# One Silu on ScalarE in place of a tanh and a VectorE product, for the gates of both layers

## The chip, the cores and the metric

The kernel runs on one core of a Trainium2 chip. The metric is the time of one execution on the device, in microseconds (us). A second source is one execution under the hardware profiler: its span goes from the first to the last instruction of the program, and all rows with durations come from it. The engines are called as the profile calls them: PE (TensorE's matmuls; PEld its weight loads), DVE (VectorE), ACT (ScalarE), POOL (GpSimd) and SP (SyncE, which issues the DMAs).

## The reference

Two layers, each a residual: x + W_out(mixer(RMSNorm(x)) * silu(gate)), on 256 positions of width 2048. The gate comes from the layer's one input projection, so it carries the row's norm factor as the other projections do.

```python
def mla_layer(x, ...):                       # layer A
    z = rms_norm(x, norm_g) @ w_in
    cq, ckv, k_pe, gate = jnp.split(z, ...)
    ...
    o = mla_attend(q, k, v, pos)             # 16 heads, softmax with a chunk-causal mask
    return x + (o * jax.nn.silu(gate)) @ w_out

def diff_layer(x, ...):                      # layer B
    z = rms_norm(x, norm_g) @ w_in
    q, k, v, gate = jnp.split(z, ...)
    ...
    o = diff_attend(q, k, v, pos, lam)       # 8 heads, difference of two softmaxes
    o = rms_norm(o, subln_g) * (1.0 - lam_init)
    return x + (o * jax.nn.silu(gate)) @ w_out
```

silu(g) = g * sigmoid(g) = (g / 2) * (1 + tanh(g / 2)).

## The kernel before, in words

The 256 rows are two tiles of 128. All products are made in three matmuls of split operands (mm3, lines 122 to 125): a high part, rounded to the fp32r type, and a low part, the remainder. Weights are streamed from HBM in chunks of two contraction tiles of 128 rows (project, line 127). For each chunk (stream, line 105) a DMA fills `raw`, ACT casts it into `whi` (line 118), and DVE subtracts to give `wlo` (line 119); PE then runs 12 matmuls on the chunk. There are four buffers of `raw` and three each of `whi` and `wlo`, so ACT can cast a chunk only once PE has finished with the one three before it.

The row's norm factor (r0 in layer A, r1x in layer B) is not applied to x. It is applied to what comes out of the projections. The gate's accumulator in PSUM holds g / r0. Before the change, ACT computes tanh(acc * r0h) with r0h = r0 / 2 (line 354 in layer A, line 668 in layer B), DVE adds one and multiplies by the accumulator (lines 355 and 669), and the factor r0h that is still missing enters elsewhere: in layer A in the scaling of the softmax by the reciprocal of its sum (line 474, its second scalar per row), in layer B in the factor f that scales the heads' output (line 722).

Layer A works on pairs of heads (hp = 0 to 7). For each: k_up and q_up project keys, values and queries, head_t transposes them, soft_a makes the scores and the softmax (DVE takes the row's extreme at line 468, ACT the Exp at line 470, DVE the scaling at line 474), p_a transposes the probabilities `e` (line 484), av_a multiplies by the values and by the transposed gate. In between, fill(i) puts chunks of the gate's projection, gate_mm, or of the output projection. The gate has four blocks (gb = 0 to 3) of 512 columns; each ends with the two activations of line 354, one for each row tile, and gate_t transposes the result later. Block 0 is finished ahead of the first softmax, blocks 1, 2 and 3 behind the last chunk put into pairs 0, 2 and 4.

Layer B works on 8 heads. For each: qk_b projects queries and keys, vg_b values and gate (eight chunks), and within vg_b's chunks stand qk_t, soft_b (scores, Exp at line 688, scaling at lines 690 to 692) and p_b, which transposes the probabilities `eb` (line 703). Behind the last chunk of vg_b come the values' split (line 151, tiles vhb and vlb) and the gate's two activations (line 668). av_b and go_b follow among the chunks of the next head's qk_b.

The program gives the instructions in this order, but each engine's own order is settled by the tile framework when it schedules the program: the Exp of line 619, for one, is written behind layer A and runs during its first projection. Each engine runs its list in order. The profile has two table loads on ACT (ACT_TABLE_LOAD): one that line 77 asks for by name, and one at line 619 that the program does not write and the framework put in.

Of the kernel before, what the change touches and what calls it, by code (L numbers as in the profile page):

```python
# [9 lines left out]
F32 = mybir.dt.float32  # L10
# [3 lines left out]
AF = mybir.ActivationFunctionType  # L14
ALU = mybir.AluOpType
# [3 lines left out]
P = 128  # L19
S = 256  # L20
NT = S // P
# [15 lines left out]
BV = 256  # L37
# [17 lines left out]
def hybrid_kernel(ctx: ExitStack, tc: tile.TileContext, x, xT, pos, posc, rows, gains, wz, wgA, wqu, wkvu, woA, wB, woB, out):  # L55
# [18 lines left out]

# [1 line left out]
    gains_t = const.tile([P, 2 * KD + 14], F32, tag="gains", name="gains_t")  # L76
# [16 lines left out]

    # keep the tensor engine's clock up while the first operands arrive
    wsrc = const.tile([P, 512], BF16, tag="wsrc", name="wsrc")
# [4 lines left out]

# [1 line left out]
    state = {}  # L102
# [24 lines left out]
    def project(accs, lhs, blocks, w, c0, c1, nk):  # L127
        """accs[b][t] += lhs(k, t) . weights of block b, for the chunks c0..c1 of two contraction tiles each."""
        for c in range(c0, c1):
            ws = [stream(b[c], 2 * w) for b in blocks]  # L130
            for kk in range(2):
                k = 2 * c + kk
                for (hi, lo), acc in zip(ws, accs):
                    for t in range(NT):
                        xh, xl = lhs(k, t)
                        mm3(acc[t], xh, xl, hi[:, kk * w:(kk + 1) * w], lo[:, kk * w:(kk + 1) * w],
                            k == 0, k == nk - 1)
# [7 lines left out]

# [1 line left out]
    xh = big.tile([P, KD, S], F32R, tag="xh", name="xh")  # L147
# [49 lines left out]

    # mean square of each row of x, and its root's reciprocal
    r0 = const.tile([P, NT], F32, tag="r0", name="r0")
# [9 lines left out]
    rsqrt(r0, msx)  # L209
    r0h = const.tile([P, NT], F32, tag="r0h", name="r0h")  # L210
    V.tensor_scalar(r0h, r0, 0.5, None, ALU.mult)
    r0sq = const.tile([P, NT], F32, tag="r0sq", name="r0sq")
    V.reciprocal(r0sq, msx)

# [1 line left out]
    posr_t = prow[:, 0, :]  # L216
# [25 lines left out]
    A.activation(cos_, kk_, AF.Sin)  # L242
    # ropc[q|k]: cosines, rops: signed sines, both times the gain of the element they multiply
    V.tensor_scalar(gqkr_t[:, 1, :], gqkr_t[:, 1, :], math.sqrt(AQK), None, ALU.mult)
# [31 lines left out]

    # lambda, on every partition
    lamp = sm.tile([P, 2, HD], F32, tag="junk", name="lamp", bufs=1)
# [5 lines left out]

# [1 line left out]
    m16 = big.tile([P, 2, 2, 4, S], F32R, tag="m16", name="m16")  # L286
# [5 lines left out]
    def latents():  # L292
        ss = sm.tile([P, NT, 2, 2], F32, tag="ssl", name="ss", bufs=1)
        for t in range(NT):
            junk = sm.tile([P, 512], F32, tag="junk", name="junk", bufs=1)
            for i in range(2):
                for j, (b, c0, w, o0) in enumerate(pieces[i]):
                    A.activation(junk[:, :w], zacc[b][t][:, c0:c0 + w], AF.Square, accum_out=ss[:, t, i, j:j + 1])
        mean = sm.tile([P, NT, 2], F32, tag="ml", name="mean", bufs=1)
        V.tensor_reduce(mean, ss, AX.X, ALU.add)  # L300
        V.tensor_tensor(mean, mean, bc(r0sq, 2), ALU.mult)
        V.tensor_scalar(mean, mean, 1.0 / LORA, EPS, ALU.mult, ALU.add)
        sig = sm.tile([P, NT, 2], F32, tag="sig", name="sig", bufs=1)
        rsqrt(sig.rearrange("p a b -> p (a b)"), mean.rearrange("p a b -> p (a b)"))
        V.tensor_tensor(sig, sig, bc(r0, 2), ALU.mult)
        for t in range(NT):
            cn = att.tile([P, 2, LORA], F32, tag="gT", name="cn")
            for i in (1, 0):
                for b, c0, w, o0 in pieces[i]:
                    V.tensor_scalar(cn[:, i, o0:o0 + w], zacc[b][t][:, c0:c0 + w], sig[:, t, i:i + 1], None, ALU.mult)  # L310
            cns.append(cn)
        # shared rotary key: its square sum, and its rotated form with the gain
        kp = sm.tile([P, NT, ROPE], F32, tag="kp", name="kp", bufs=1)
        k2 = sm.tile([P, NT, ROPE], F32, tag="k2", name="k2", bufs=1)
        for t in range(NT):
            V.tensor_scalar(kp[:, t], zacc[2][t][:, 256:320], r0[:, t:t + 1], None, ALU.mult)
            junk = sm.tile([P, 512], F32, tag="junk", name="junk", bufs=1)
            A.activation(junk[:, :ROPE], kp[:, t], AF.Square, accum_out=sskp[:, t:t + 1])
        V.tensor_tensor(krope, kp, ropc[:, 1], ALU.mult)
        V.tensor_tensor(k2[:, :, :HR], kp[:, :, HR:], rops[:, 1, :, :HR], ALU.mult)  # L320
        V.tensor_tensor(k2[:, :, HR:], kp[:, :, :HR], rops[:, 1, :, HR:], ALU.mult)
        V.tensor_tensor(krope, krope, k2, ALU.add)
        V.tensor_scalar(sskp, sskp, AQK * EPS, None, ALU.add)
# [15 lines left out]

# [1 line left out]
    KC = KD // 2  # L341
# [4 lines left out]
    def gate_mm(gb, c0, c1):  # L346
        if c0 == 0:
            gate_acc(gb)
        project([state["ga", gb]], feat(xh, xl), [wgA[gb]], 512, c0, c1, KD)
        if c1 == KC:  # L350
            sgs = []
            for t, acc in enumerate(state.pop(("ga", gb))):
                sg = sm.tile([P, 512], F32, tag="sg", name="sg", bufs=2)
                A.activation(sg, acc, AF.Tanh, scale=r0h[:, t:t + 1])
                V.scalar_tensor_tensor(sg, sg, 1.0, acc, ALU.add, ALU.mult)
                sgs.append(sg)
            state["sg", gb] = sgs
# [10 lines left out]
    def k_up(hp):  # L368
        """keys, normalised, and values of two heads"""
        ka = pair(psu)  # L370
# [23 lines left out]
    def q_up(hp):  # L394
        """queries of two heads, not scaled: their norm enters with the scores"""
        kn, rt, ss, f, vh, vl = state["k", hp]
# [25 lines left out]
    def head_t(hp):  # L422
        kn, rt, ss, f, vh, vl = state.pop(("k", hp))
        qn = state.pop(("q", hp))
        tiles = []
# [10 lines left out]
        for i in (1, 0):  # L436
            for t in range(NT):
                T.transpose(pt[:, i, t * P:(t + 1) * P], rt[:, i, t].rearrange("p h d -> p (h d)"), ident)
        # each head's rotary rows: q as [hi; lo], k's hi and lo twice over, so that every product has 128 rows
        q2 = att.tile([P, 2, S], F32R, tag="q2", name="q2")  # L440
# [12 lines left out]
    def soft_a(hp):  # L453
# [9 lines left out]
        for h, ps in enumerate(pss):  # L463
            e = sm.tile([P, NT, S], F32, tag="e", name="e", bufs=2)
            mx = sm.tile([P, NT], F32, tag="mx", name="mx")
            den = sm.tile([P, NT], F32, tag="den", name="den")
            for t in range(NT):
                V.tensor_tensor_reduce(e[:, t, :], ps[:, t, :], maskA[:, t, :], f[:, 0, t, h:h + 1], 3e38,
                                       ALU.add, ALU.min, mx[:, t:t + 1])
                A.activation(e[:, t, :], e[:, t, :], AF.Exp, bias=mx[:, t:t + 1], scale=-1.0,  # L470
                             accum_out=den[:, t:t + 1])
            V.reciprocal(den, den)
            for t in range(NT):
                V.tensor_scalar(e[:, t, :], e[:, t, :], den[:, t:t + 1], r0h[:, t:t + 1], ALU.mult, ALU.mult)
            es.append(e)
# [81 lines left out]

# [1 line left out]
    x1 = big.tile([P, NT, D], F32, tag="m16", name="x1")  # L559
# [56 lines left out]
    rsqrt(r1x, m1)  # L616
    r1h = const.tile([P, NT], F32, tag="r1h", name="r1h")
    V.tensor_scalar(r1h, r1x, 0.5, None, ALU.mult)
    A.activation(lams, lams, AF.Exp)
# [5 lines left out]

# [1 line left out]
    def qk_b(h, c0, c1):  # L627
# [30 lines left out]
    def vg_b(h, c0, c1):  # L658
# [8 lines left out]
        for t in range(NT):  # L667
            A.activation(sg[:, t, :], acc[t][:, BV:], AF.Tanh, scale=r1h[:, t:t + 1])
            V.scalar_tensor_tensor(sg[:, t, :], sg[:, t, :], 1.0, acc[t][:, BV:], ALU.add, ALU.mult)
        state["vgb", h] = (vh, vl, sg)  # L670
# [36 lines left out]
    def av_b(h):  # L707
# [13 lines left out]
        rsqrt(f, ss)  # L721
        V.tensor_tensor(f, f, r1h, ALU.mult)
        go = att.tile([P, NT, BV], F32, tag="go", name="gob", bufs=1)
# [35 lines left out]

# [1 line left out]
    def finish_b(n, t, c0, c1):  # L761
# [20 lines left out]
def _columns(w, width):  # L782
    """(K, N) -> (N / width, K / 256, 128, 2 * width): blocks of columns in chunks of two row tiles."""
    k, n = w.shape
# [48 lines left out]
```

## Time and profile before

| | |
|---|---|
| time, median of 3 runs (lowest, highest) | 847.49 us (846.46, 847.53) |
| span of the profiled execution (its own time beside it is not given) | 845.0 us |
| instructions | 11706 |
| PE busy | 835.9 us, 99% of the span |
| DVE busy | 564.6 us, 67% |
| ACT busy | 488.0 us, 58% |
| POOL busy | 86.4 us, 10% |
| read from and written to HBM | 145.73 MB and 2.10 MB |

A row of the groups by line gives line, engine, operation, tiles written <- read, their shapes and the count, then the busy time in us and the mean of one in ns, and last the engine's idle time just before them and what ended most of it. A row of a timeline gives the start in us from the span's beginning, the duration in us, engine, line, operation, tiles and count (consecutive instructions of a kind are one row), and in brackets the idle time before it with its releaser. The end of a matmul in the profile is modelled, so that consecutive matmuls overlap in it. Idle time of an engine that is not the bottleneck costs nothing by itself.

### The profile page before, as it was taken

The numbers are of one execution on the slowest core, as the hardware profiler recorded it, in microseconds if no ns is written. First come the engines' busy times: TensorE is split into PE (matmuls) and PEld (weight loads), VectorE is DVE, ScalarE is ACT, GpSimd is POOL, SyncE is SP. The second block draws the span as 40 slices with busy tenths as digits, with TensorE's granted clock in tenths as the row PEclk, the third lists the DMA queues.
The fourth block names the chain that finished last, engine by engine and source line by source line (L and its number), as shares of the span: only waits on it lengthen the run. The fifth ranks groups of instructions, "written<-read, shape, count | busy, mean of one in ns | idle before, by whom it ended". The sixth has DMA issues, their size and how long they took to land.

```text
span 845.0 us, 11706 instructions
## 1 busy us (share of the span) xinstructions
PE 835.9 (99%) x4187; PEld 714.5 (85%) x4187; DVE 564.6 (67%) x968; ACT 488.0 (58%) x995; POOL 86.4 (10%) x113
## 2 busy tenths in 40 slices
PE   8999999999999999999999999999999999999998
PEld 6988888889888888888888888888888888888886
DVE  6968678788787866555647565565756566565543
ACT  7656687677767656555555465555555564554331
POOL 2300221122202200000010010010001000000000
PEclk9999999999999999999999999999999999999999
DMA  8755544534444645555555555554555555455661
GB/s 268 256 197 162 166 147 146 176 116 162 144 144 149 248 154 180 180 186 177 185 175 174 175 175 175 175 175 150 193 181 175 175 175 171 168 184 198 219 211 70
DMA packets 42954, 148.59 MB, mean 176 GB/s; under 512 B 5008, under 2 KB 6032, under 8 KB 42640
## 3 DMA queue, kind: packets, MB, share of 16 engines
q1 hardware_dynamic: 42896, 147.84, 52.5%
q8 instruction: 33, 0.54, 0.3%
q14 instruction: 25, 0.20, 0.1%
HBM read 145.73 MB, written 2.10 MB: 175 GB/s over the span
## 4 chain that ended last, share of the span: by engine, by line
PE 94%; DVE 3%; DMA 1%; ACT 1%; issue 0%; SPq 0%; POOL 0%; DVEq 0%; ACTq 0%
PE pu L123 14%; PE pu L125 14%; PE pu L124 14%; PE pg L124 13%; PE pg L123 13%; PE pg L125 13%; DVE wlo L119 1%; PE ptb L651 1%; PE ptn L430 1%; PE ptp L484 1%; PE pa L124 1%; DMA raw<-in_wz 1%; PE pa L125 1%; PE pa L123 1%; DVE xl L152 1%; PE ps L462 0%
## 5 line engine op out<-in xcount | busy, mean ns | idle before, releaser
L119 DVE TENSOR_TENSOR wlo<-raw,whi 128x1024 fp32r<-128x1024 f32 (+4 forms) x278 | 328.6, 1191 | 189.8 <-ACT whi L118 189.5
L118 ACT CAST whi<-raw 128x1024 fp32r<-128x1024 f32 (+3 forms) x277 | 282.2, 1025 | 233.6 <-PE pg L125 102.6
L123 PE MATMUL pu<-whi,x1h 128*128 128x512 f32 x256 | 101.3, 396 | 0.0
L123 PE MATMUL pg<-whi,x1h 128*128 128x512 f32 x256 | 100.5, 392 | 0.0
L125 PE MATMUL pu<-whi,x1l 128*128 128x512 f32 x256 | 99.9, 390 | 0.0
L124 PE MATMUL pu<-wlo,x1h 128*128 128x512 f32 x256 | 99.8, 390 | 0.0
L124 PE MATMUL pg<-wlo,x1h 128*128 128x512 f32 x256 | 99.7, 390 | 0.0
L125 PE MATMUL pg<-whi,x1l 128*128 128x512 f32 x256 | 99.7, 389 | 0.0
L125 PEld LDWEIGHTS pu<-whi,x1l 128*128 128x128 f32 x256 | 48.1, 188 | 10.2
L125 PEld LDWEIGHTS pg<-whi,x1l 128*128 128x128 f32 x256 | 48.1, 188 | 10.1
L123 PEld LDWEIGHTS pg<-whi,x1h 128*128 128x128 f32 x256 | 48.1, 188 | 9.5
L124 PEld LDWEIGHTS pg<-wlo,x1h 128*128 128x128 f32 x256 | 48.1, 188 | 9.4
L124 PEld LDWEIGHTS pu<-wlo,x1h 128*128 128x128 f32 x256 | 48.2, 188 | 9.2
L123 PEld LDWEIGHTS pu<-whi,x1h 128*128 128x128 f32 x256 | 48.1, 188 | 9.2
L123 PE MATMUL pg<-whi,xh 128*128 128x512 f32 (+1 forms) x128 | 49.8, 391 | 1.9 <-ACT whi L118 1.3
L124 PE MATMUL pg<-wlo,xh 128*128 128x512 f32 (+1 forms) x128 | 48.7, 381 | 1.9 <-DVE wlo L119 1.9
L123 PE MATMUL pg<-whi,goh 128*128 128x512 f32 x128 | 50.5, 395 | 0.0
L123 PE MATMUL pu<-whi,goh 128*128 128x512 f32 x128 | 50.1, 392 | 0.0
L124 PE MATMUL pg<-wlo,goh 128*128 128x512 f32 x128 | 49.9, 390 | 0.0
L125 PE MATMUL pg<-whi,gol 128*128 128x512 f32 x128 | 49.9, 390 | 0.0
L124 PE MATMUL pu<-wlo,goh 128*128 128x512 f32 x128 | 49.9, 390 | 0.0
L125 PE MATMUL pu<-whi,gol 128*128 128x512 f32 x128 | 49.9, 389 | 0.0
(246 smaller groups left out, 1551.1 us busy)
## 6 DMA issues: line engine op xcount, KB each, us to landing
raw<-in_wB SPq DMA_DIRECT2D x128, 512.0 KB, 3.2
raw<-in_wgA SPq DMA_DIRECT2D x32, 512.0 KB, 3.5
raw<-in_woA SPq DMA_DIRECT2D x32, 512.0 KB, 3.3
raw<-in_woB SPq DMA_DIRECT2D x32, 512.0 KB, 3.2
raw<-in_wkvu SPq DMA_DIRECT2D x16, 512.0 KB, 4.3
raw<-in_wz SPq DMA_DIRECT2D x15, 544.0 KB, 5.7
raw<-in_wqu SPq DMA_DIRECT2D x16, 384.0 KB, 3.1
x<-in_x SPq DMA_DIRECT2D x1, 2048.0 KB, 10.0
```

The costliest lines, as they stand in the source:

```text
L118: (V.tensor_copy if after_first and a == 0 else A.copy)(hi[:, a:b], raw[:, a:b])
L119: V.tensor_tensor(lo[:, a:b], raw[:, a:b], f32(hi[:, a:b]), ALU.subtract)
L123: T.matmul(o, shi, mhi, start=start, stop=False)
L124: T.matmul(o, shi, mlo, start=False, stop=False)
L125: T.matmul(o, slo, mhi, start=False, stop=stop)
L152: V.scalar_tensor_tensor(lo, src, g, f32(hi), ALU.mult, ALU.subtract)
L430: T.transpose(pt[:, h, t * P:(t + 1) * P], src[:, t, h, :NOPE], ident)
L484: T.transpose(pt[:, c, t * P:(t + 1) * P], e[:, t, c * P:(c + 1) * P], ident)
L651: T.transpose(pt[:, m, t * P:(t + 1) * P], qk[:, t, 2 * i + m, :], ident)
```

## The change

The gate's two steps become one activation, Silu, that reads the accumulator with the full norm factor as its scale per row. The factors r0h and r1h, which carried the half, and the places where they entered go away. Nothing else in the program is changed but comments, which are left out here.

```diff
     rsqrt(r0, msx)
-    r0h = const.tile([P, NT], F32, tag="r0h", name="r0h")
-    V.tensor_scalar(r0h, r0, 0.5, None, ALU.mult)
...
                 sg = sm.tile([P, 512], F32, tag="sg", name="sg", bufs=2)
-                A.activation(sg, acc, AF.Tanh, scale=r0h[:, t:t + 1])
-                V.scalar_tensor_tensor(sg, sg, 1.0, acc, ALU.add, ALU.mult)
+                A.activation(sg, acc, AF.Silu, scale=r0[:, t:t + 1])
...
             for t in range(NT):
-                V.tensor_scalar(e[:, t, :], e[:, t, :], den[:, t:t + 1], r0h[:, t:t + 1], ALU.mult, ALU.mult)
+                V.tensor_scalar(e[:, t, :], e[:, t, :], den[:, t:t + 1], None, ALU.mult)
...
     rsqrt(r1x, m1)
-    r1h = const.tile([P, NT], F32, tag="r1h", name="r1h")
-    V.tensor_scalar(r1h, r1x, 0.5, None, ALU.mult)
...
         for t in range(NT):
-            A.activation(sg[:, t, :], acc[t][:, BV:], AF.Tanh, scale=r1h[:, t:t + 1])
-            V.scalar_tensor_tensor(sg[:, t, :], sg[:, t, :], 1.0, acc[t][:, BV:], ALU.add, ALU.mult)
+            A.activation(sg[:, t, :], acc[t][:, BV:], AF.Silu, scale=r1x[:, t:t + 1])
...
         rsqrt(f, ss)
-        V.tensor_tensor(f, f, r1h, ALU.mult)
```

## The prediction

> **What bounds the kernel now.** I read the page first, then the busy time by stage, then the timelines around the gates. Three lines of the page:
>
> ```profile
> span 845.0 us, 11706 instructions
> PE 835.9 (99%) x4187; PEld 714.5 (85%) x4187; DVE 564.6 (67%) x968; ACT 488.0 (58%) x995; POOL 86.4 (10%) x113
> PE 94%; DVE 3%; DMA 1%; ACT 1%; issue 0%; SPq 0%; POOL 0%; DVEq 0%; ACTq 0%
> ```
>
> TensorE (PE) has work in 99% of the span and is 94% of the chain that ended last; ScalarE (ACT) and VectorE (DVE), the engines that the change touches, are busy 58% and 67%. An average can hide a stage, so the next view is the busy time in five stretches. Its columns are the length, then the busy time of PE, of PE's weight loads, of DVE, ACT and POOL, each with its instructions, then the granted clock.
>
> ```profile
> 0.00:62.00 62.00, 56.99 (x318) 52.49 (x319) 48.11 (x106) 39.44 (x71) 13.66 (x16) 1.00 0.71 240
> 62.00:80.00 18.00, 17.85 (x87) 14.44 (x86) 15.51 (x36) 10.51 (x24) 0.04 (x1) 1.00 0.54 172
> 80.00:395.00 315.00, 315.00 (x1666) 274.14 (x1665) 231.94 (x423) 207.41 (x474) 46.85 (x76) 1.00 0.50 165
> 395.00:790.00 395.00, 395.00 (x1896) 331.43 (x1895) 244.39 (x380) 213.33 (x412) 25.88 (x21) 1.00 0.52 176
> 790.00:845.00 55.00, 51.09 (x226) 41.99 (x224) 24.68 (x24) 17.32 (x17) 0.00 (x0) 1.00 0.50 163
> ```
>
> From 80 to 790 us, which holds every gate, both softmaxes and all the products that the change edits, PE is busy for 710.00 of 710.00 us at a granted clock of 1.00. There is no wait there for the change to remove. What work it takes from DVE or adds to ACT reaches the end only if it makes PE wait where PE now waits for nothing. So the question is one of room: how late may ACT and DVE be before a matmul or a transpose finds its operand missing?
>
> The span is 845.0 us and the timed runs' median is 847.49, 2.5 us more; the profiled execution has no time of its own beside its span. I take differences of the span and add them to 847.49.
>
> **What the edits cost by themselves.** The groups of instructions by line, ACT first and then DVE (busy us in total, mean ns of one, idle before them):
>
> ```profile
> L668 ACT ACTIVATE sgb<-pu,r1h 128x256 f32<-128x256 f32 x16 | 7.6, 473 | 0.0
> L354 ACT ACTIVATE sg<-pg,r0h 128x512 f32<-128x512 f32 x6 | 3.8, 685 | 0.1
> L151 ACT ACTIVATE vhb<-pu,r1x 128x256 fp32r<-128x256 f32 x16 | 7.6, 474 | 9.3 <-PE pu L125 9.3
> L470 ACT ACTIVATE e<-e,mx 128x256 f32<-128x256 f32 x32 | 16.0, 502 | 15.5 <-DVE mx L468 15.5
> L688 ACT ACTIVATE eb<-eb,mxb 128x256 f32<-128x256 f32 x32 | 15.9, 500 | 1.1
> L77 ACT ACT_TABLE_LOAD x1 | 1.3, 1283 | 0.7 <-PEq L826 0.7
> ```
>
> ```profile
> L355 DVE SCALAR_TENSOR_TENSOR sg<-sg,pg 128x512 f32<-128x512 f32 x6 | 3.9, 685 | 0.1
> L669 DVE SCALAR_TENSOR_TENSOR sgb<-sgb,pu 128x256 f32<-128x256 f32 x16 | 6.6, 413 | 0.0
> L474 DVE TENSOR_SCALAR e<-e,den,r0h 128x256 f32<-128x256 f32 x32 | 11.8, 412 | 0.6
> L272 DVE TENSOR_SCALAR distB<-rowf,posf 128x256 f32<-128x256 f32 x2 | 0.7, 342 | 0.0
> L722 DVE TENSOR_TENSOR fo<-fo,r1h 128x2 f32<-128x2 f32 x8 | 1.3, 161 | 6.5 <-POOL fo L92 6.5
> ```
>
> Silu in place of Tanh: the same 24 activations from PSUM with a scale per row. Tanh (L668, 473 ns) and a scaled copy of the same shape (L151, 474 ns) cost the same, so I give Silu the 473 and 685 ns of Tanh: nothing changes.
>
> Taken from DVE: the gate's product, 8 in layer A at 685 ns (six are in the row, the first gate's two I take alike) and 16 in layer B at 413 ns, 5.5 + 6.6 = 12.1 us; eight products with r1h, 1.3 us; two single ones that made r0h and r1h, some 0.3 us by the price of L722. L474 loses its second scalar: L272 is a product of this shape with one scalar per row, 342 ns, so 70 ns less for each of 32, 2.2 us. In sum DVE falls by 15.9 us to about 549 us. None of it is on PE's path, since PE waits for nothing there: worth 0 us. The start, where PE has its only early idle time, has no gate: of these edits only the one on r0h (before 60 us) comes near it, and PE idles 0.15 us in the whole stretch from 62 to 80, so the gain is between 0 and 0.15 us. I take 0.1 and forecast 847.4.
>
> **What the diff does not show.** ACT evaluates its functions from a table that has to be loaded. [...]
>
> ```profile
> 39.80 0.62 ACT L188 ACTIVATE sq<-xs 128x512 f32<-128x512 f32 x1
> 40.44 1.28 ACT L619 ACT_TABLE_LOAD   x1
> 43.56 0.20 ACT L619 ACTIVATE lams<-lams 128x2 f32<-128x2 f32 x1 [1.84 <-DVE lams L281]
> ```
>
> After that, 64 more Exps (L470, L688) alternate with 24 Tanhs to the end of the kernel without another load. So Exp's set has Tanh, and silu's set, with which the kernel began, has no Exp, else L619 would need none. I take it that Silu is not in Exp's set. Then every change between the two functions is a load on ACT. Counting the places in the code: layer A has four gates, each with a load before its Silus and another before the next Exp, 8; layer B has one gate for each of 8 heads, between the Exps of its head and those of the next, 8 loads plus 7. That is 23 loads more, 25 in all, 23 x 1.283 = 29.5 us, and ACT rises from 488 to about 517.5 us. The row above also shows that a load need not wait for what its activation waits for: it starts 0.02 us after the instruction ahead of it, and is over 1.84 us before its Exp. What stands behind each load on ACT are the weight casts (L118), without which PE stops, and the softmax.
>
> How much room is there? Layer B, Exps of the second head (timelines of ACT, of DVE, of PE):
>
> ```profile
> 452.34 1.05 ACT L118 CAST whi<-raw 128x1024 fp32r<-128x1024 f32 x1 [1.67 <-PE pu L125]
> 453.52 0.51 ACT L688 ACTIVATE eb<-eb,mxb 128x256 f32<-128x256 f32 x1
> ```
>
> ```profile
> 456.55 0.87 DVE L692 SCALAR_TENSOR_TENSOR eb<-eb,denb 128x256 f32<-128x256 f32 x2
> ```
>
> ```profile
> 459.04 0.60 PE L703 MATMUL ptpb<-ident,eb 128*128 128x128 f32 x4
> ```
>
> The cast ends at 453.39, so a load that follows it 0.02 us later ends at 454.69 and the Exp is 1.17 us late. The result of the softmax was ready at 457.42, and PE turned to it at 459.04: room 1.62 us, 0.45 left. Without the load that Exp starts 0.13 us after the cast, so next to nothing of the load is hidden in front of it; the room behind it hides it. The other load of a head, in front of the Silu:
>
> ```profile
> 462.82 0.47 ACT L668 ACTIVATE sgb<-pu,r1h 128x256 f32<-128x256 f32 x1
> 463.18 1.05 ACT L118 CAST whi<-raw 128x1024 fp32r<-128x1024 f32 x1
> ```
>
> ```profile
> 464.26 1.23 DVE L119 TENSOR_TENSOR wlo<-raw,whi 128x1024 fp32r<-128x1024 f32 x1 [0.49 <-ACT whi L118]
> ```
>
> ```profile
> 469.36 0.40 PE L124 MATMUL pg<-wlo,x1h 128*128 128x512 f32 x1
> ```
>
> The cast behind it becomes 1.3 us late; its low half was done at 465.49 and used at 469.36, room 3.87.
>
> Layer A is tighter, because there the load before Silu is followed some 6 us later by the load before Exp (three times, at gates 1 to 3). The first time, ACT, DVE and PE:
>
> ```profile
> 133.35 1.27 ACT L354 ACTIVATE sg<-pg,r0h 128x512 f32<-128x512 f32 x2
> 134.50 1.78 ACT L118 CAST whi<-raw 128x1024 fp32r<-128x1024 f32 x2
> 136.41 0.28 ACT L380 ACTIVATE junk<-pu 128x128 f32<-128x128 f32 x1
> ...
> 138.40 0.20 ACT L380 ACTIVATION_READ_ACCUMULATOR junk<-pu 128x1 f32 x1
> 139.43 0.51 ACT L470 ACTIVATE e<-e,mx 128x256 f32<-128x256 f32 x1 [0.84 <-DVE mx L468]
> ...
> 140.57 0.71 ACT L155 CAST vh<-pu 128x256 fp32r<-128x256 f32 x2 [0.54 <-DVE kn L387]
> ```
>
> ```profile
> 144.19 0.74 DVE L474 TENSOR_SCALAR e<-e,den,r0h 128x256 f32<-128x256 f32 x2
> 144.94 2.36 DVE L119 TENSOR_TENSOR wlo<-raw,whi 128x1024 fp32r<-128x1024 f32 x2
> ```
>
> ```profile
> 146.22 1.03 PE L484 MATMUL ptp<-ident,e 128*128 128x128 f32 x8
> ...
> 147.32 0.40 PE L124 MATMUL pg<-wlo,xh 128*128 128x512 f32 x1
> ```
>
> The Silu pair starts 1.28 us late, and so do the casts; between them and the squares (L380) lie 0.13 us of idle time, so the squares are 1.15 late, and all that hangs on them, the copy vh (L155) among it. The second load starts at 138.60 + 1.15 and ends at 141.03; its Exp is then 1.60 us late and with its read over at 141.63, but vh's operand comes at 140.57 + 1.15 = 141.72 anyway: the second load is hidden. DVE arrives at the four products of L474 1.15 us late, gains 4 x 0.07 = 0.28 there, and is 0.87 late at the two low halves (L119). The first of the pair was done at about 146.12 (half of 2.36 after 144.94) and PE took it at 147.32: room 1.2, 0.33 left. The transposes of e have 146.22 - 144.93 = 1.29. So none of the 23 loads reaches PE: 0 us, by a margin of 0.33 us at three places and 0.45 at seven.
>
> This rests on a load costing 1.28 us and no more; the trace bounds it. Below, it is the record itself. Above, ACT was idle for 1.84 us between the load at L619 and its Exp; the profile puts that down to DVE, but a pause of ACT's own would be covered by it, so up to 1.28 + 1.84 = 3.12. I take 1.28, the only duration recorded. The Trainium skill, page "ScalarE: Activation LUTs", section "What ACT_TABLE_LOAD costs", states the same 1283 ns, but adds a drain of 1380 ns, 2.66 us for every switch; no run so far shows that drain. Its section on table sets says to batch activations by set, which the present kernel does and the changed one would not.
>
> **The rivals.**
> *A pause behind each load (slower).* With a load of x us, the casts and squares at gates 1 to 3 are x - 0.13 late, and the second load adds x - 1.37 (138.60 + x + 0.60 for the Exp and its read, against 140.57); PE is reached when the sum passes 1.2 + 0.28 = 1.48, that is from x = 1.49. In layer B it is reached when x - 0.11 passes 1.62, from x = 1.73. At 3.12 PE loses 2.99 + 1.75 - 1.48 = 3.26 us three times and 3.01 - 1.62 = 1.39 seven times, 19.5 us: 867. For it: nothing in the trace has ACT start work right after a load. Against it: the idle time has another releaser. By the page's 2.66 us the same sum would be 13.5 us, 861.
> *The order spends the room (slower by little).* The order on each engine is not the program's: L619 is written behind layer A and runs at 43.56 us. A planner that weighs the longer ACT may place the casts so that neither load at gates 1 to 3 is hidden: 2 x 1.28 - 1.48 = 1.08 us three times, 3.2 us: 850.6.
> *The lead-in shortens (faster).* PE idles 62 - 56.99 = 5.0 us in the first 62 us, and a new order could recover some of it; two fifths would give 845.4. Against it: the edits begin behind that stretch.
> *The loads do not come.* If Exp's set holds Silu, the change only frees DVE: 847.4 as well.
>
> **How the numbers follow.** A measurement of this kernel can tell about 0.2% (1.7 us) from no change. Forecast 847.4: 0.70. No loads, same time: 0.04. Order spends the room, 850.6: 0.08. A pause, up to 867: 0.12. Lead-in, 845.4: 0.06. So within 0.2%: 0.74; slower: 0.20; faster: 0.06. The range 846.0 to 850.8 takes in the two cases at 847.4, which hold most of the chance, and the one at 850.6, and leaves out the pause and the faster case.
>
> **What the changed profile would show.** Right: 25 table loads of 1.28 us with the next activation directly behind at least some of them; ACT near 517, DVE near 549; PE still busy all the way from 80 to 790; Silu at 473 and 685 ns, L474's successor at 342. Wrong: PE idle in front of L703, or in front of L124 behind the softmax of layer A, three or seven times over; ACT idle by more than 0.1 us behind loads whose operands were ready.

## The result, and the profile after

| | before | after |
|---|---|---|
| time, median (lowest, highest; runs) | 847.51 us (846.46, 847.55; 4) | 853.81 us (853.27, 854.02; 4) |
| span of the profiled execution (its own time) | 845.0 us | 852.2 us (854.02 us) |
| DVE busy | 564.6 us | 549.2 us |
| ACT busy | 488.0 us | 516.9 us |

The ratio after to before is 1.0078, with a 95% interval of 1.0065 to 1.0091: the change makes the kernel 6.3 us slower. The forecast was 847.4, with a range up to 850.8.

The page of the changed kernel, and two of the five stretches:

```profile
span 852.2 us, 11693 instructions
PE 837.3 (98%) x4187; PEld 714.2 (84%) x4187; DVE 549.2 (64%) x934; ACT 516.9 (61%) x1018; POOL 83.4 (10%) x113
PE 82%; DVE 8%; ACT 5%; issue 2%; DMA 1%; POOL 1%; SPq 0%; DVEq 0%; ACTq 0%
```

```profile
80.00:395.00 315.00, 309.37 (x1636) 268.16 (x1636) 220.15 (x410) 213.04 (x463) 42.43 (x75) 1.00 0.49 161
395.00:790.00 395.00, 395.00 (x1895) 331.23 (x1894) 238.34 (x358) 234.04 (x442) 27.50 (x22) 1.00 0.53 176
```

The stretch with layer B's gates is still full (395.00 of 395.00). The stretch of layer A, which was full before, has 5.63 us without a matmul. The list of PE's waits names what ended them (us in total, times, longest):

```profile
PE pu L123 <- DVE vl L156: 5.6, 4, 1.7
```

PE waits four times for `vl`, the low half of the values, to start a product that writes `pu`. The four products in the timeline of PE, first before the change, then after it:

```profile
115.37 0.33 PE L123 MATMUL pu<-whi,m 128*128 128x384 f32 x1
...
142.03 0.33 PE L123 MATMUL pu<-whi,m 128*128 128x384 f32 x1
...
196.20 0.33 PE L123 MATMUL pu<-whi,m 128*128 128x384 f32 x1
...
250.38 0.33 PE L123 MATMUL pu<-whi,m 128*128 128x384 f32 x1
```

```profile
116.65 0.41 PE L123 MATMUL pu<-whi,m 128*128 128x384 f32 x1 [1.01 <-DVE vl L156]
...
144.79 0.41 PE L123 MATMUL pu<-whi,m 128*128 128x384 f32 x1 [1.23 <-DVE vl L156]
...
200.94 0.41 PE L123 MATMUL pu<-whi,m 128*128 128x384 f32 x1 [1.70 <-DVE vl L156]
...
257.09 0.41 PE L123 MATMUL pu<-whi,m 128*128 128x384 f32 x1 [1.69 <-DVE vl L156]
```

They are the first matmuls of q_up for pairs 1, 2, 4 and 6, and they come 1.28, 2.76, 4.74 and 6.71 us later than before: each adds its own loss, and with the fourth 6.7 of the 7.2 us by which the span grew are reached. (The bracket is shorter than the loss because the matmul ahead of it is drawn some 0.15 us beyond the issue of the next one.) The tag `pu` has two banks. k_up of a pair fills both with keys and values, and q_up of the same pair needs the same two banks, so its first product can't start before the last reader of k_up's values in the first bank is done. That reader is the first of the two vl.

Why is vl late? DVE's timeline at pair 1, before and after:

```profile
113.69 0.76 DVE L387 TENSOR_TENSOR kn<-pu,fq 128x256 f32<-128x256 f32 x2 [0.60 <-POOL fq L92]
...
114.56 0.75 DVE L156 TENSOR_TENSOR vl<-pu,vh 128x256 fp32r<-128x256 f32 x2
...
115.42 0.48 DVE L468 CUSTOM_DVE_ANT_0 e<-ps,maskA,fq 128x256 f32<-128x256 f32 x1
```

```profile
113.79 0.76 DVE L384 TENSOR_TENSOR kn<-pu,fq 128x256 f32<-128x256 f32 x2 [0.60 <-POOL fq L92]
...
114.86 0.48 DVE L465 CUSTOM_DVE_ANT_0 e<-ps,maskA,fq 128x256 f32<-128x256 f32 x1
...
115.67 0.49 DVE L465 CUSTOM_DVE_ANT_0 e<-ps,maskA,fq 128x256 f32<-128x256 f32 x1
...
116.08 0.76 DVE L156 TENSOR_TENSOR vl<-pu,vh 128x256 fp32r<-128x256 f32 x2
```

kn, ahead of it, is only 0.10 us later, but vl is 1.52 us later: it now stands behind three reductions of the softmax (L465, formerly L468) that used to stand behind it. DVE's list has another order, though no line of the source that concerns vl was touched. ACT, which feeds vl, shows that the load did not hold it up here:

```profile
112.30 1.28 ACT L467 ACT_TABLE_LOAD   x1
113.59 0.51 ACT L467 ACTIVATE e<-e,mx 128x256 f32<-128x256 f32 x1
...
114.25 0.70 ACT L155 CAST vh<-pu 128x256 fp32r<-128x256 f32 x2
```

vh comes at 114.25 (114.14 before), as soon as the first kn is done, as before. The order moved in this way at pairs 1, 2, 4 and 6 and not at pairs 3, 5 and 7. The softmax that runs beside k_up of a pair is that of the pair ahead (0, 1, 3 and 5 for the four), and just these four softmaxes have a table load in front of their first Exp.

The groups by line show that the edits themselves cost what they were given, and where the loads are:

```profile
L663 ACT ACT_TABLE_LOAD x8 | 10.3, 1283 | 0.1
L682 ACT ACT_TABLE_LOAD x7 | 9.0, 1283 | 0.1
L352 ACT ACT_TABLE_LOAD x4 | 5.1, 1283 | 0.8 <-PE pa L125 0.7
L467 ACT ACT_TABLE_LOAD x4 | 5.1, 1283 | 0.1
L663 ACT ACTIVATE sgb<-pu,r1x 128x256 f32<-128x256 f32 x16 | 6.7, 471 | 0.1
L352 ACT ACTIVATE sg<-pg,r 128x512 f32<-128x512 f32 x6 | 3.8, 686 | 0.0
```

### The profile page after: what moved, and what is told of

The parts are those of the page before. It is cut to its first block, busy times and chain, and to the rows that moved or that the text cites. A ratio compares the mean times of both kernels' runs of the same rounds, so it can differ in the third digit from the quotient of the medians.

```text
span 852.2 us, 11693 instructions
## 1 busy us (share of the span) xinstructions
PE 837.3 (98%) x4187; PEld 714.2 (84%) x4187; DVE 549.2 (64%) x934; ACT 516.9 (61%) x1018; POOL 83.4 (10%) x113
## 4 chain that ended last, share of the span: by engine, by line
PE 82%; DVE 8%; ACT 5%; issue 2%; DMA 1%; POOL 1%; SPq 0%; DVEq 0%; ACTq 0%
PE pu L123 13%; PE pu L125 13%; PE pu L124 12%; PE pg L124 12%; PE pg L125 12%; PE pg L123 11%; DVE wlo L119 3%; ACT whi L118 2%; DVE xl L152 1%; DMA raw<-in_wz 1%; PE ptb L646 1%; POOL fq L92 1%; PE pa L124 1%; PE pa L125 1%; DVE nl L152 1%
## 5 line engine op out<-in xcount | busy, mean ns | idle before, releaser
L124 PE MATMUL pu<-wlo,x1h 128*128 128x512 f32 x256 | 99.8, 390 | 0.0
L124 PE MATMUL pg<-wlo,x1h 128*128 128x512 f32 x256 | 99.7, 390 | 0.0
L124 PEld LDWEIGHTS pg<-wlo,x1h 128*128 128x128 f32 x256 | 48.1, 188 | 9.5
L124 PEld LDWEIGHTS pu<-wlo,x1h 128*128 128x128 f32 x256 | 48.2, 188 | 9.2
L123 PE MATMUL pu<-whi,m 128*128 128x384 f32 (+1 forms) x128 | 46.7, 365 | 5.6 <-DVE vl L156 5.6
L124 PE MATMUL pg<-wlo,xh 128*128 128x512 f32 (+1 forms) x128 | 48.6, 380 | 1.5 <-DVE wlo L119 1.3
L124 PE MATMUL pg<-wlo,goh 128*128 128x512 f32 x128 | 49.8, 389 | 0.0
```

Of the source, the lines that this page charges most:

```text
L123: T.matmul(o, shi, mhi, start=start, stop=False)
L124: T.matmul(o, shi, mlo, start=False, stop=False)
```

## The experiments

Two theories stood at the start. Theory L: the loads delay ACT, and PE with it. Theory O: the loads are hidden for the most part, and the planned order, which the loads changed, costs the time. (The planner is the part of the tile framework that sets each engine's order.) Times are medians of five or more runs, each beside the kernel before on the same chip (847.39 us for the first four, 846.94 for the next four, 846.92 for the last three); ratios are to that, with the 95% interval. In the diffs, `after(a, b)` stands for a dependency added by hand that puts instruction a behind b in the order of its engine and makes it wait for nothing.

**1. The change with vl pinned to its old place.**

```diff
 def k_up(hp): ...
-            split(vh[:, t], vl[:, t], k3[:, :, NOPE:])
+            A.copy(vh[:, t], k3[:, :, NOPE:])
+            state["vl", hp] = V.tensor_tensor(vl[:, t], k3[:, :, NOPE:], f32(vh[:, t]), ALU.subtract)
 def soft_a(hp): ...
-                V.tensor_tensor_reduce(e[:, t, :], ps[:, t, :], maskA[:, t, :], ...)
+                r = V.tensor_tensor_reduce(e[:, t, :], ps[:, t, :], maskA[:, t, :], ...)
+                if hp + 1 < NP and h + t > 0:
+                    after(r, state["vl", hp + 1])
```

> The change with all its 23 added table loads, but with DVE's order in layer A pinned as it was before: the low half of the values (vl) ahead of the last three softmax reductions of the pair, where the changed kernel has it behind them for pairs 1, 2, 4 and 6. Theory O (the loads themselves are hidden for the most part; the time went into the moved vl, which holds the two pu banks that the next q_up needs): the four waits of 1.2 to 2.0 us in front of q_up go or shrink; at pairs 2, 4 and 6 the load before Silu may still leave up to 0.7 us each, so 847.5 to 849.6. Theory L (the loads delay ACT, and any order would show it): 853 to 854, as the change.

850.36 us, ratio 1.0038 (1.0024 to 1.0052). The wait for vl shrinks from 5.6 us to 0.9, but there is a new one at the transposes of e, and the loss halves where it should all but go. Neither theory holds alone. The planner reacted to the pin: it put the low halves of the next weights ahead of the second head's products of e and the transposes of e in two parts. PE's order is therefore not that of before, and the waits listed are less than the 3.0 us lost. Two of PE's waits:

```profile
PE pu L123 <- DVE vl L386: 0.9, 2, 0.5
PE ptp L484 <- DVE e L474: 0.4, 2, 0.2
```

**2. The kernel before, with vl moved, and no load.**

```diff
 def k_up(hp): ...
-            split(vh[:, t], vl[:, t], k3[:, :, NOPE:])
+            if hp in (1, 2, 4, 6):       # vh here, vl in soft_a, behind its last reduction
+                A.copy(vh[:, t], k3[:, :, NOPE:])
+                state["vl", hp, t] = lambda t=t, k3=k3: V.tensor_tensor(vl[:, t], ...)
+            else:
+                split(vh[:, t], vl[:, t], k3[:, :, NOPE:])
```

> The kernel before (Tanh and product, no load added), with one thing of the changed kernel: for pairs 1, 2, 4 and 6 the low half of the values stands on DVE behind the last three softmax reductions. Three reductions take 1.2 us; by the rows of before the first vl then ends 1.0 us too late for q_up at pair 1 and 0.75 us at pairs 2, 4 and 6. Theory O: 3.2 us slower, 850.7, with waits of PE for vl at these four places. Theory L: no load, no loss, 847.5.

851.78 us, ratio 1.0049 (1.0036 to 1.0062): 4.4 us lost without a single load, with the same four waits:

```profile
PE pu L123 <- DVE vl L390: 3.5, 4, 1.0
```

The order alone costs, somewhat more than forecast. It is not quite the order of the changed kernel: the second vl of each of these pairs stands two products of e further back, but the four waits are for the first (at pair 1 it starts at 115.39 and takes 0.41 us, and PE starts at 115.94). Together with the first run: the order and the delay each cost something, and they overlap (4.4 and 3.0 against 6.3 for both).

**3 and 4. One layer at a time.** The change in layer A alone, so that layer B goes back to these lines; and in layer B alone, with the like in layer A.

```diff
-            A.activation(sg[:, t, :], acc[t][:, BV:], AF.Silu, scale=r1x[:, t:t + 1])
+            A.activation(sg[:, t, :], acc[t][:, BV:], AF.Tanh, scale=r1h[:, t:t + 1])
+            V.scalar_tensor_tensor(sg[:, t, :], sg[:, t, :], 1.0, acc[t][:, BV:], ALU.add, ALU.mult)
...
+        V.tensor_tensor(f, f, r1h, ALU.mult)
```

> The change in layer A alone; layer B keeps Tanh and product. Both theories place the whole loss in layer A: 853.5 to 854.0, 8 added loads. If the 15 loads of layer B cost anything: below that by as much.

> The change in layer B alone; layer A keeps Tanh and product. By the room of 1.62 us in front of the transposes of the probabilities, 15 loads of 1.28 us cost nothing: 847.5, PE busy without a gap from 80 us on. If they cost something that the profile of the changed kernel does not show as a wait: above 848.5.

Layer A alone: 853.67 us, ratio 1.0075 (1.0061 to 1.0088). Layer B alone: 847.06 us, ratio 0.9998 (0.9989 to 1.0007), with 15 loads of 1283 ns among its rows. All of the loss is in layer A; layer B's loads cost nothing that can be told.

**5. The change without its loads.** Leaves out the gate's product: the gate enters as tanh(g).

```diff
-                A.activation(sg, acc, AF.Silu, scale=r0[:, t:t + 1])
+                A.activation(sg, acc, AF.Tanh, scale=r0[:, t:t + 1])
...
-            A.activation(sg[:, t, :], acc[t][:, BV:], AF.Silu, scale=r1x[:, t:t + 1])
+            A.activation(sg[:, t, :], acc[t][:, BV:], AF.Tanh, scale=r1x[:, t:t + 1])
```

> The change with Tanh put where it has Silu: what is taken from DVE stays away, no table load is added. Leaves out the gate's product: the gate enters as tanh(g) and not as silu(g). If DVE's relief is worth nothing and the loads cause the whole loss, by delay or through the planned order: 847.4, no wait of PE from 80 us on. If DVE's 16 us are worth something that the loads hid: below 845.7.

847.39 us, ratio 1.0006 (0.9998 to 1.0015). DVE is down to 550.9 us and the time stays. What the change takes from DVE is worth nothing, and without loads there is no loss and vl stays in place.

**6. DVE pinned as before in both places.** As in 1, and the low halves of the weights streamed behind p_a stand behind the last product of e.

```diff
 def soft_a(hp): ...
-                V.tensor_scalar(e[:, t, :], e[:, t, :], den[:, t:t + 1], None, ALU.mult)
+                state["laste"] = V.tensor_scalar(e[:, t, :], e[:, t, :], den[:, t:t + 1], None, ALU.mult)
 def p_a(hp): ...
+        state["pin"] = state["laste"]
 def stream(...): ...
-            V.tensor_tensor(lo[:, a:b], raw[:, a:b], f32(hi[:, a:b]), ALU.subtract)
+            r = V.tensor_tensor(lo[:, a:b], raw[:, a:b], f32(hi[:, a:b]), ALU.subtract)
+            if "pin" in state:
+                after(r, state["pin"])
```

> The change with DVE's order in layer A as before in both places that moved in the first of these runs: vl ahead of the last three reductions, and the low halves of the next weights (wlo) behind the last product of e. PE's order is then that of before. What is left is the delay that the loads make in a fixed order: the load before Silu pushes the squares, vh and vl at pairs 2, 4 and 6; the run with vl pinned shows 0.6 us at q_up for it at pairs 4 and 6, and 0.2 to 0.5 us at the transposes of e, which should go. So 3 x 0.65 = 2 us: 849.4. If delay in a fixed order cost nothing: 847.4; if the pinned wlo does not matter: 850.4 again.

849.78 us, ratio 1.0035 (1.0023 to 1.0048), near the 849.4 expected. PE's order is that of before; on DVE one small product, rt, now stands ahead of vl at these pairs. Three waits for vl are left, at pairs 2, 4 and 6, and none at pair 1:

```profile
PE pu L125 <- DVE vl L388: 1.7, 3, 0.8
```

So this is the delay that the loads make with vl and the next low halves in their old places.

**7. vh pinned ahead of the first Exp on ACT.**

```diff
 def soft_a(hp): ...
-                A.activation(e[:, t, :], e[:, t, :], AF.Exp, bias=mx[:, t:t + 1], scale=-1.0, ...)
+                x_ = A.activation(e[:, t, :], e[:, t, :], AF.Exp, bias=mx[:, t:t + 1], scale=-1.0, ...)
+                if hp + 1 in (1, 2, 4, 6):
+                    after(x_, state["vh", hp + 1])
```

> The change with one thing pinned on ACT at pairs 1, 2, 4 and 6: the cast vh stands ahead of the first Exp of the softmax and of its table load, where the others have it behind. With that alone the planner gives DVE and PE the order of before. The load before Exp then comes behind vh, and delays the four Exps by some 1.9 us against 1.29 of room at the transposes of e. Theory (the loss needs vh behind a loaded Exp in the planned order): the big waits of 1.2 to 2.0 us at q_up go; what stays is the load before Silu, up to 0.65 us at pairs 2, 4 and 6, and up to 0.4 us at the transposes of e in four pairs: 848.5 to 850.5. If the order of DVE had not been settled by this, 853.8.

850.61 us, ratio 1.0042 (1.0030 to 1.0055), just past the upper end. With this pin on ACT alone, the orders of PE and of DVE's work on the pairs are those of before again. So the planner moved vl only where vh stood behind an Exp with a load. Again the waits for vl are at pairs 2, 4 and 6 only; they are drawn as 1.6 of the 3.7 us, and from 62 us on the list has one other, of 0.2 us:

```profile
PE pu L123 <- DVE vl L386: 1.6, 3, 1.0
```

These three have what pair 1 has not: a load in front of the gate's Silus, just ahead of the weight casts and the squares from which kn, vh and vl follow.

**8. Two loads in a row in layer B.**

```diff
 def soft_b(h): ...
+                if t == 0 and m == 0:
+                    dm = sm.tile([P, 1], F32, tag="dm", name="dm")
+                    dmi = A.activation(dm, mx[:, 0:1], AF.Silu)      # unused
-                A.activation(e[:, m, :], e[:, m, :], AF.Exp, ...)
+                x_ = A.activation(e[:, m, :], e[:, m, :], AF.Exp, ...)
+                after(x_, dmi)
```

> The kernel before (Tanh and product) with one Silu of 128x1 elements, whose result nothing uses, in front of the Exps of each head of layer B: two table loads back to back there, 16 in all. It tests the room of 1.62 us in front of the transposes of the probabilities, which one load (1.17 us late) did not use up. Two loads and the small activation make the Exps 2.7 us late: if that room is what hid the loads, PE waits there in each of 8 heads, by 0.3 us where the transposes are planned in two halves and up to 1.1 us where not, 2 to 9 us in all: 850 to 856. If something else hid them (the planner moving work): 847.5.

847.49 us, ratio 1.0004 (0.9995 to 1.0014): the second branch of the expectation, that something other than the room hides them. ACT's timeline at the second head shows the delay that was asked for:

```profile
453.96 1.28 ACT L690 ACT_TABLE_LOAD   x1
455.26 0.20 ACT L690 ACTIVATE dm<-mxb 128x1 f32<-128x1 f32 x1
455.47 1.28 ACT L691 ACT_TABLE_LOAD   x1
456.76 0.51 ACT L691 ACTIVATE eb<-eb,mxb 128x256 f32<-128x256 f32 x1
```

DVE and PE in the same stretch:

```profile
458.54 0.49 DVE L696 SCALAR_TENSOR_TENSOR eb<-eb,denb 128x256 f32<-128x256 f32 x1
...
459.59 0.48 DVE L696 SCALAR_TENSOR_TENSOR eb<-eb,denb 128x256 f32<-128x256 f32 x1
```

```profile
459.60 0.38 PE L707 MATMUL ptpb<-ident,eb 128*128 128x128 f32 x2
459.74 0.48 PE L123 MATMUL pu<-whi,x1h 128*128 128x512 f32 x1
460.05 0.39 PE L124 MATMUL pu<-wlo,x1h 128*128 128x512 f32 x1
460.28 0.38 PE L707 MATMUL ptpb<-ident,eb 128*128 128x128 f32 x2
```

The plan gave way: DVE finishes the first tile of eb by itself (ready at 459.03), and PE takes the transposes in two pairs with two weight matmuls between, the second after the second tile (460.07). Reading room off the old plan overstates the loss where PE has other work to put in between.

**9. Silu's table loaded early, nothing pinned.** A Silu of one element per partition in head_t of pairs 1, 3 and 5, ahead of the end of gates 1, 2 and 3:

```diff
             split_gain(hi, lo, pt, gqk_t[:, i:i + 1])
+            if i == 0 and hp in (1, 3, 5):
+                A.activation(sm.tile([P, 1], F32, tag="dm", name="dm"), f32(hi[:, 0, 0:1]), AF.Silu)   # unused
```

> The change, with a Silu of 128x1 elements (result unused) in head_t ahead of gates 1, 2 and 3, so that silu's table is loaded some 6 us earlier, where ACT idles, and the gate's own Silus find it; number of loads as in the change. Nothing is pinned, and DVE's planned order still has vl behind the three reductions at pairs 1, 2, 4 and 6. If the loss is made of the moved vl (4.4 us by the run that moved it alone) and, at pairs 2, 4 and 6, of the load in front of Silu, only the second part goes: 851 to 852. If the place of that load does not matter: 853.8.

851.75 us, ratio 1.0056 (1.0042 to 1.0069), as expected: a loss of 4.8 us where the change has 6.3, and what stays is the moved vl (four waits, 3.3 us in all).

**10 and 11. The early load together with a pin.** Run 9's edit with that of 7, and with that of 6.

> The early load of silu's table together with the cast vh pinned ahead of the first Exp on ACT at pairs 1, 2, 4 and 6, which gives DVE and PE the order of before. With vh pinned alone the loss was 3 us, all of it at pairs 2, 4 and 6, none at pair 1, where no load stands in front of the squares. If that load is what was left, it goes: 847.2 to 848.5, all 25 loads (and the change's whole saving on DVE) in place. If the load before the Exps is the rest: 850 again.

> The early load of silu's table together with DVE's order pinned as before (vl ahead of the reductions, the next low halves behind the products of e). Pinned alone, this left waits of 0.6 to 0.9 us at pairs 2, 4 and 6 and none at pair 1. If the load in front of the squares made them: 847.2 to 848. If the late Exps made them: 849.8 again.

847.74 us, ratio 1.0011 (1.0002 to 1.0020), and 847.70 us, ratio 1.0008 (1.0000 to 1.0017). Of the 6.3 us some 0.8 are left, in intervals that begin at or just above 1, and every load is still made. PE's stretch of layer A in run 10, and ACT there:

```profile
80.00:395.00 315.00, 315.00 (x1665) 273.72 (x1664) 223.63 (x414) 216.28 (x484) 47.34 (x76) 1.00 0.50 165
```

```profile
125.79 1.28 ACT L434 ACT_TABLE_LOAD   x1
127.09 0.20 ACT L434 ACTIVATE dm<-nh 128x1 f32<-128x1 f32 x1
128.92 0.37 ACT L448 CAST kh<-ptr 64x256 fp32r<-64x256 f32 x1 [1.63 <-DVE q L447]
...
133.46 1.27 ACT L352 ACTIVATE sg<-pg,r 128x512 f32<-128x512 f32 x2
```

The load at 125.79 uses time in which ACT waited for DVE anyway; the Silus at 133.46 need none. No version beat the kernel before: PE is full from 80 to 790 us in the best of them, as it was.

## Why the prediction was wrong, point by point

**What bounds the kernel: right.** From 80 to 790 us PE has no idle time to give back; without the loads (run 5) the time is that of before.

**The prices of the edits: right.** Silu takes 471 and 686 ns (473 and 685 forecast), DVE is busy 549.2 us (549) and ACT 516.9 us (517). The scaling that replaced L474 takes 351 ns, not 342.

**The loads: right in number and price.** 25 loads of 1283 ns. None of the 23 added ones has a pause behind it: the next activation starts 0.01 us after its load, as at 113.59 in the changed kernel and, in run 8, at 456.76. So the rival of a pause fell with the changed profile. The Trainium skill, page "ScalarE: Activation LUTs", section "What ACT_TABLE_LOAD costs", gives 1283 ns and a drain of 1380 ns for every switch; the first agrees with these rows and the second does not appear in them, and the measurement decides. The rule to batch activations by set, which the same page of the Trainium skill gives under "Table sets: the hidden batching unit", is borne out in layer A only, through what the loads did to the order and the delay; in layer B 15 switches more cost nothing that can be told.

**The room: this step failed.** The claim that none of the 23 loads reaches PE, by a margin of 0.33 us in layer A, left out the tightest reader. The prediction said that in layer A "the squares are 1.15 late, and all that hangs on them, the copy vh (L155) among it", and went on to ask only whether the weights' low halves and the transposes of e would be late. It named vh and did not ask who waits for it. vl reads vh, vl is the last reader of the two pu banks, and q_up needs these banks. In the kernel before, the row of vl at pair 2, where a load before Silu stands in front of the squares, is this:

```profile
140.98 0.75 DVE L156 TENSOR_TENSOR vl<-pu,vh 128x256 fp32r<-128x256 f32 x2
```

One vl takes 0.42 us, so the first of the two ended at 141.40, and q_up started at 142.03: 0.6 us. In the changed kernel at pair 1 the first vl ended at 116.50 and PE, which waited for it, started at 116.65; with these 0.15 us taken off, the room was about 0.5 us. Against that stands the lateness of 1.15 us, and it was sized rightly. Run 6 at the same place, on ACT, DVE and PE:

```profile
143.68 0.70 ACT L387 CAST vh<-pu 128x256 fp32r<-128x256 f32 x2
```

```profile
144.30 0.75 DVE L388 TENSOR_TENSOR vl<-pu,vh 128x256 fp32r<-128x256 f32 x2
```

```profile
144.86 0.41 PE L125 MATMUL pu<-whi,m 128*128 128x384 f32 x1 [0.76 <-DVE vl L388]
```

That execution was 1.9 us behind already (q_up of pair 1 started at 117.24, before at 115.37). So vh is 1.2 us late (143.68 against 140.57), and q_up 0.9 (144.86 against 142.03): what the room doesn't hide, and 0.2 more because rt stands ahead of vl. In the two runs with vl in its old place and PE's order that of before (6 and 7) the loss is 2.8 and 3.7 us. Runs 10 and 11 bring the load before Silu forward and keep the one before the Exps, and 0.8 us is left. The signs of being wrong that the prediction named, PE idle in front of L703 or of L124, did not come; PE was idle in front of q_up.

**The order: the second part of the same step.** The sum was made in the old order. The rival "the order spends the room" named the right kind of thing, gave it 0.08, and priced it by the weight casts at 850.6. What the planner moved was vl, at four places, and that alone costs 4.4 us (run 2). Why its reckoning did so is not seen in any profile; what is shown is that the order moves when an Exp with a load stands ahead of vh on ACT (run 7 undoes it), and that on the chip the load did not delay vh at pair 1.

**Layer B: right, with more room than forecast.** No loss (run 4), and PE's order there is that of before, so the room did hide the loads. The second head in the changed kernel, on DVE and PE:

```profile
463.40 0.49 DVE L686 SCALAR_TENSOR_TENSOR eb<-eb,denb 128x256 f32<-128x256 f32 x1
...
464.44 0.48 DVE L686 SCALAR_TENSOR_TENSOR eb<-eb,denb 128x256 f32<-128x256 f32 x1
```

```profile
465.97 0.60 PE L697 MATMUL ptpb<-ident,eb 128*128 128x128 f32 x4
```

The softmax was ready at 464.92, 1.0 us ahead of PE where 0.45 was forecast: DVE now finishes one tile before the other, where it took both together before. Nor is this room a limit, since twice the load cost nothing either, with PE's order changed (run 8).

The two parts do not add: 4.4 for the order, 2.8 for the delay in the old order, 6.3 together. Two reasons are argued, not tested: at pairs 2, 4 and 6 a vl that comes late by its place in the list hides part of the lateness of vh, and a PE that has lost time gives ACT time to catch up. How much is due to each is open.

## What to carry to other kernels

Before an activation is exchanged, see which table the others between need: here one function in place of two cost 23 loads, and the function that it replaced shared its table with Exp. When you ask whether a delay is hidden, follow every reader of the late tile up to the buffer that it frees, not only the operands of the next matmul; and where a planner orders the program, compare the order of every engine before and after, since an added instruction on one engine can move another engine's work. A load that can't be avoided can be hidden by a tiny use of its function that brings it forward into time in which the engine waits anyway; here that, with the order kept, took the loss from 6.3 us to 0.8.

## What the runs showed of the hardware that was not expected

The granted clock in the first microseconds differs between executions. The stretch from 14 to 19 us in the profile of run 6, and in that of the kernel before:

```profile
14.00:19.00 5.00, 4.82 (x20) 4.82 (x21) 4.66 (x7) 3.62 (x7) 1.38 (x1) 0.66 0.95 337
```

```profile
14.00:19.00 5.00, 5.00 (x30) 5.00 (x31) 4.97 (x6) 5.00 (x9) 1.39 (x1) 1.00 0.99 348
```

At a mean of 0.66 PE does 20 matmuls in the time of 30. That execution took 851.66 us where the median of its kernel is 849.78, and its first q_up came 1.9 us later than in the kernel before (95.44 against 93.58): a single execution can be off by a third of this change's effect, for a reason far from the change.
